# Power on GpSimd for the memory norms, an earlier order of the token norms, and memory attention by token halves, in a hybrid decoder layer

## The chip, the core and the metric

One core of one Trainium2 chip runs the whole layer in one launch. The time is that of the device in microseconds, the median of repeated runs of the same program; the profile is one further execution, recorded by the hardware profiler. The engines are named as in the profile: PE (TensorE), DVE (VectorE), ACT (ScalarE), POOL (GpSimd), and SP, whose queue issues the transfers here.

## The reference

One decoder layer on x of 1024 tokens by 1024 channels and a memory of 256 tokens, all float32:

```python
h = rmsnorm(x, norm_g)
pool_v, pool_gate, sb_q, sb_k, sb_v, sb_gate, mem_q, mem_gate = split(h @ w_in)
y_pool = pool_mixer(pool_v) * silu(pool_gate)
y_sb = stick_breaking_attention(sb_q, sb_k, sb_v) * silu(sb_gate)   # 8 heads of 64
mem_k, mem_v = split(rmsnorm(mem, mem_norm_g) @ w_mem_kv)
s = rmsnorm(mem_q, per head) @ rmsnorm(mem_k, per head).T * 64**-0.5  # 4 heads
y_mem = softmax(s) @ mem_v * silu(mem_gate)
out = x + concat(y_pool, y_sb, y_mem) @ w_out
```

An rmsnorm multiplies by (mean of squares + 1e-6) to the power -1/2. The pooling divides sums over windows of 2 to 16 tokens by the number of tokens in the window.

## The kernel before

Every product is made in three matmuls: an operand is split into a high part that ACT rounds and a low part that DVE or POOL gets by subtraction, and high by high, high by low and low by high are summed in PSUM. A projection of 128 output channels is a "unit" (u_q0, u_k0, u_v0, u_g0 for the first of four pairs of stick-breaking heads, and so on). It has two halves of 512 tokens, each of eight steps, one for each 128 input channels; a step is three matmuls of 512 columns (L208, L211). A unit's weights come through one single buffer, wr: SP loads it, ACT makes the high part (wh, L150), POOL the low part in four pieces (wl, L154), and only then can the next unit's load begin.

The program goes in stages:

- Start. The memory (m) is transposed and multiplied by its key and value weights (kv_step). Each of the eight token tiles (x0 to x7, 128 tokens each) is normalised: ACT squares and sums, DVE makes mean plus epsilon (root, L124), POOL raises it to -1/2 (L125), DVE refines it by a Newton step (L129, L130) and scales the tile (L135), or POOL scales it for tiles 4 and 5. h_step transposes one block of 128 channels of four tiles on PE (tx, L381), and ACT and DVE split it into hh and hl. A half needs all four of its tiles before its first block is done.
- Memory queries. The units mq0 and mq1 make four heads' queries into G0 to G3; ACT squares them (sqq), PE sums the squares of each head by a product with a matrix of two columns (sp, L553), and rsqrt_cols turns the sums into factors (qsc). The memory keys get the same norm (kv_root, kv_newton) and are transposed (km_step: tk on PE, then four operations on ACT and four on DVE).
- Memory attention (mem_main). It has 16 items, one for each pair of heads, head and 256 tokens. An item makes scores (z_m, L576, a bank of the two named z), their negative maximum on DVE (L578) and its product with qsc (L583), two exponentials on ACT (L587), the division of one half on POOL and one on DVE (L598), four transpositions (ta_m, L495), the split (ah_m, al_m), and the product with the values (av). The second use of a z bank waits for the exponentials of the item before the last.
- Four stick-breaking pairs (sb_main), whose chain runs from z over a sigmoid on ACT, a scan on DVE (L651), transpositions and splits to av; and then the output product.

In both attentions PE would wait for that chain. So `weave` mixes the items' steps (main) with steps of later units (fill): it takes fill steps until the time that its own cost table gives for the next main step, and leaves the last `keep` fill steps for the end. How many fill steps a stage gets is set by `cut`, and what is left goes to the first stick-breaking pair. PE's order is the program's order everywhere. The order of ACT, DVE and POOL is the program's up to start.close(), and is made by the scheduler of the framework from there on. Each engine works through its own list in that order, and an instruction that waits holds up those behind it.

Of the kernel before, what the change touches and what calls it, by code (L numbers as in the profile page):

```python
# [8 lines left out]
F32 = mybir.dt.float32  # L9
F32R = mybir.dt.float32r  # L10
AF = mybir.ActivationFunctionType
# [14 lines left out]
def layer_kernel(  # L26
# [56 lines left out]
    mhalf = const.tile([P, 1], F32, name="mhalf")  # L83
# [6 lines left out]
    def rsqrt_cols(ss, n, inv, name):  # L90
# [4 lines left out]
        nc.scalar.activation(t[:, :n], v[:, :n], AF.Sqrt)  # L95
        nc.scalar.activation(spare[:, 0:1], t[:, 0:1], AF.Copy)
        nc.vector.reciprocal(r[:, :n], t[:, :n])
# [464 lines left out]
    def mem_main(mq, ys):  # L562
        items = [(pr, h, j) for pr in range(2) for h in range(2) for j in range(NT // 2)]
        box = {}

        def qk(it):
# [15 lines left out]
            for i in range(2):  # L582
                nc.vector.tensor_scalar_mul(nb[:, 2 + i : 3 + i], nb[:, i : i + 1], qsc[:, c0 + 2 * i : c0 + 2 * i + 1])  # L583
# [197 lines left out]
    nc.scalar.activation(spare[:, 0:1], mhalf[:, 0:1], AF.Square)  # L781
# [3 lines left out]
    )  # L785
    warm(tm[0], 10)
# [12 lines left out]
    for kk in range(1, 4):  # L799
        xn[kk - 1].square()  # L800
        xn[kk - 1].root()
        kv_split(kk)
        xn[kk - 1].newton()
        xn[kk - 1].scale(nc.vector)
        if kk < 3:
            m_evac(kk + 1)
        kv_step(kk)
# [3 lines left out]
    xn[3].square()  # L811
    xn[3].root()
    xn[3].newton()
    xn[3].scale(nc.vector, slice(0, 512))
    w_mq = [(slot("wh", f"wh_mq{pr}", dt=F32R), slot("wl", f"wl_mq{pr}", dt=F32R)) for pr in range(2)]
# [25 lines left out]
    xn[4].square()  # L841
    xn[4].root()
# [13 lines left out]
    for k in range(KD):  # L856
        half[0, 0][k][1]()
        half[1, 0][k][1]()
        if k + 3 < KD:
            h_step(0, k + 3)  # L860
        if k >= 5:
            h_step(1, k - 5)
        if k == 0:
            for i in range(2):
                mn[i].newton(col=rm[:, i : i + 1])
        if k <= 3:
            xn[4 + k].newton()
        if k < 3:
            xn[5 + k].square()
            xn[5 + k].root()  # L870
        if k <= 3:
            xn[4 + k].scale(nc.gpsimd if k < 2 else nc.vector)
        if k == 3:
            u_q[0].weights()
        if k == 4:
            kv_evac()
# [10 lines left out]
    cnt = const.tile([P, 32], F32, name="cnt")  # L887
    for r in range(2):
        nc.gpsimd.iota(
            cnt[:, r * 16 : r * 16 + 16],  # L890
            pattern=[[1, 16]],
            base=1,
            channel_multiplier=0,
            allow_small_or_imprecise_dtypes=True,
        )
        for h in range(2):
            w = 2 << (2 * r + h)
            rows = slice(h * HD, (h + 1) * HD)
            nc.vector.tensor_scalar_min(cnt[rows, r * 16 : r * 16 + 16], cnt[rows, r * 16 : r * 16 + 16], float(w))
    nc.vector.reciprocal(cnt[:], cnt[:])  # L900

    for k in range(KD):
        half[0, 1][k][1]()
        half[1, 1][k][1]()
        if k == 0:
            kv_root()
            kv_newton()
        if k in (4, 5):
            km_step(kmn, k - 4)
        if k in (6, 7):  # L910
            mem_ss(k - 6, 0)
    mem_scale(0)
    start.close()
    fill = u_q[0].steps[8:] + chain([u_k[0], u_v[0], u_g[0], u_q[1], u_k[1], u_v[1], u_g[1]], u_q[2])
    cut = 8 + 16 + 17 + 16 + 3
    fill, fill_0 = fill[:cut], fill[cut:]
    run(fill[:6])
    mem_ss(0, 1)
    mem_ss(1, 1)
    mem_scale(1)  # L920
    nc.scalar.activation(spare[:, 1:2], spare[:, 0:1], AF.Exp, scale=0.0)
    run(fill[6:9])
    y_mem = [slot(f"Y{pr}", f"y_mem{pr}") for pr in range(2)]
    weave(mem_main(mq, y_mem), fill[9:], 6, 1.0)
# [227 lines left out]
```

## Time and profile before

| | us |
|---|---|
| median of three runs | 530.4 (529.99 to 531.61) |
| the profiled execution, whole | 531.56 |
| its span, first to last instruction | 529.6 |
| PE busy in the span | 514.6 |
| DVE busy | 392.9 |
| ACT busy | 292.0 |
| POOL busy | 173.0 |

The profiled execution lies 1.2 us above the median of the runs, and 2.0 us of it lie outside the span. The PE column counts matmuls as busy from start to end, overlapping ones once. A PE that is busy all the time may still go at the lower of its two clocks, which the granted clock shows: 1.00 is 2.4 GHz and 0.50 is 1.2 GHz.

### The profile page before, as it was taken

The numbers are of one execution on the slowest core, as the hardware profiler recorded it, in microseconds if no ns is written. First come the engines' busy times: TensorE is split into PE (matmuls) and PEld (weight loads), VectorE is DVE, ScalarE is ACT, GpSimd is POOL, SyncE is SP. The second block draws the span as 40 slices with busy tenths as digits, with TensorE's granted clock in tenths as the row PEclk, the third lists the DMA queues.
The fourth block names the chain that finished last, engine by engine and source line by source line (L and its number), as shares of the span: only waits on it lengthen the run. The fifth ranks groups of instructions, "written<-read, shape, count | busy, mean of one in ns | idle before, by whom it ended". The sixth has DMA issues, their size and how long they took to land.

```text
span 529.6 us, 7486 instructions
## 1 busy us (share of the span) xinstructions
PE 514.6 (97%) x2716; PEld 431.3 (81%) x2716; DVE 392.9 (74%) x654; ACT 292.0 (55%) x558; POOL 173.0 (33%) x193
## 2 busy tenths in 40 slices
PE   7899999899999999999999999999999999999997
PEld 6677788787888888888888888888788888888886
DVE  3776768787587764876766777647988859999863
ACT  6777666787565554555545564535544539462400
POOL 4770133543220322022302220222345920035890
PEclk9999989999999999999999999999999999999999
DMA  8911021301111310123011113100110415414023
GB/s 304 332 45 40 2 80 40 81 1 41 41 35 46 79 41 0 41 62 94 6 40 41 41 40 80 40 27 16 40 41 0 159 48 192 158 41 153 5 112 127
DMA packets 37245, 37.25 MB, mean 70 GB/s; under 512 B 1991, under 2 KB 26841, under 8 KB 37209
## 3 DMA queue, kind: packets, MB, share of 16 engines
q1 hardware_dynamic: 37208, 36.78, 22.3%
q8 instruction: 21, 0.34, 0.3%
q14 instruction: 16, 0.12, 0.1%
HBM read 28.39 MB, written 4.19 MB: 62 GB/s over the span
## 4 chain that ended last, share of the span: by engine, by line
PE 81%; DVE 9%; ACT 3%; issue 3%; POOL 2%; DMA 2%; SPq 0%; POOLq 0%; ACTq 0%; DVEq 0%
PE av L514 8%; PE z L643 7%; PE ta L495 6%; PE u_g L211 5%; PE u_q L211 5%; PE u_k L211 5%; PE u_v L211 5%; PE u_mg L211 3%; PE oS L1034 3%; PE oS L1036 3%; PE u_pv L211 3%; PE oS L1035 3%; PE u_q L208 3%; PE u_g L208 3%; PE u_k L208 3%
## 5 line engine op out<-in xcount | busy, mean ns | idle before, releaser
L651 DVE TENSOR_TENSOR_SCAN be<-be,later 128x128 f32<-128x128 f32 (+3 forms) x64 | 91.4, 1441 | 18.7 <-ACT be L647 17.9
L500 ACT ACTIVATE ah<-ta,mone 128x512 fp32r<-128x512 f32 (+1 forms) x80 | 51.7, 646 | 56.5 <-PE ta L495 55.8
L501 DVE SCALAR_TENSOR_TENSOR al<-ta,ah 128x512 fp32r<-128x512 f32 (+1 forms) x80 | 50.7, 634 | 24.9 <-ACT ah L500 23.9
L647 ACT ACTIVATE be<-z 128x128 f32<-128x128 f32 (+3 forms) x96 | 45.8, 490 | 35.7 <-PE z L643 34.2
L495 PE MATMUL ta<-ident,be 128*128 128x128 f32 x288 | 44.8, 273 | 0.0
L495 PEld LDWEIGHTS ta<-ident,be 128*128 128x128 f32 x288 | 35.1, 140 | 7.8 <-DVE be L651 0.4
L514 PEld LDWEIGHTS av<-ah,V_v 128*128 128x128 f32 x160 | 30.0, 188 | 7.0
L514 PE MATMUL av<-al,V_v 128*128 128x256 f32 (+1 forms) x160 | 31.7, 280 | 1.1 <-DVE al L501 1.1
L514 PE MATMUL av<-ah,V_v 128*128 128x256 f32 (+1 forms) x160 | 30.0, 269 | 0.0
L208 PE MATMUL u_g<-hh,wh_g 128*128 128x512 f32 x64 | 28.0, 438 | 0.0
L208 PE MATMUL u_v<-hh,wh_v 128*128 128x512 f32 x64 | 27.4, 427 | 0.0
L154 POOL TENSOR_TENSOR wl_g<-wr_g,wh_g 128x256 fp32r<-128x256 f32 x16 | 11.9, 779 | 45.9 <-ACT wh_g L150 45.9
L154 POOL TENSOR_TENSOR wl_k<-wr_k,wh_k 128x256 fp32r<-128x256 f32 x16 | 11.5, 751 | 46.7 <-ACT wh_k L150 46.7
L208 PE MATMUL u_k<-hh,wh_k 128*128 128x512 f32 x64 | 26.7, 417 | 0.0
L154 POOL TENSOR_TENSOR wl_v<-wr_v,wh_v 128x256 fp32r<-128x256 f32 x16 | 11.3, 741 | 45.7 <-ACT wh_v L150 45.7
L1034 PE MATMUL oS<-bs,hh 128*128 128x512 f32 (+1 forms) x68 | 25.9, 381 | 0.0
L1036 PE MATMUL oS<-bs,hl 128*128 128x512 f32 (+1 forms) x68 | 25.8, 379 | 0.0
L1035 PE MATMUL oS<-bs,hh 128*128 128x512 f32 (+1 forms) x68 | 25.6, 376 | 0.0
L598 POOL TENSOR_SCALAR pe_m<-pe_m,nb_m 128x256 f32<-128x256 f32 x16 | 16.3, 1019 | 28.0 <-DVE nb_m L595 20.5
L211 PE MATMUL u_v<-hl,wh_v 128*128 128x512 f32 x64 | 25.3, 396 | 0.0
L211 PE MATMUL u_k<-hh,wl_k 128*128 128x512 f32 x64 | 25.3, 395 | 0.0
L211 PE MATMUL u_g<-hl,wh_g 128*128 128x512 f32 x64 | 25.3, 395 | 0.0
(317 smaller groups left out, 1502.1 us busy)
## 6 DMA issues: line engine op xcount, KB each, us to landing
x<-in_x_dram SPq DMA_DIRECT2D x8, 512.0 KB, 6.3
wr_q<-in_w_in_dram SPq DMA_DIRECT2D x4, 512.0 KB, 4.8
wr_k<-in_w_in_dram SPq DMA_DIRECT2D x4, 512.0 KB, 3.8
wr_v<-in_w_in_dram SPq DMA_DIRECT2D x4, 512.0 KB
wr_g<-in_w_in_dram SPq DMA_DIRECT2D x4, 512.0 KB
KA_k<-KA_k SPq DMA_DIRECT2D x8, 256.0 KB, 5.3
KB_k<-KB_k SPq DMA_DIRECT2D x8, 256.0 KB
xr<-in_x_dram SPq DMA_DIRECT2D x8, 256.0 KB, 4.0
```

The source lines that it names most:

```text
L208: nc.tensor.matmul(pt[:], wh[:, kc], hh[k][:, c], start=(k == 0), stop=False)
L211: nc.tensor.matmul(pt[:], w[:, kc], h[k][:, c], start=False, stop=(k == KD - 1 and n == 1))
L495: nc.tensor.transpose(tp[:, o : o + P], src, ident[:])
L500: nc.scalar.activation(ah[:, :w], tp[:, :w], AF.Identity, bias=mone[:, 0:1])
L501: nc.vector.scalar_tensor_tensor(al[:, :w], tp[:, :w], -1.0, f(ah[:, :w]), op0=ALU.add, op1=ALU.subtract)
L514: nc.tensor.matmul(av[:, 256 - bw : 256], vs[n], part[:, o : o + bw], start=(first and part is ah and n == 0), stop=(last and part is al a ...
L643: nc.tensor.matmul(zp[:, 0:w], q[h][:, tcol], k[h][:, n, s0 : s0 + w], start=(n == 0), stop=(n == 1))
L647: nc.scalar.activation(be[:, s0 : s0 + w], zp[:, 0:w], AF.Sigmoid, scale=-(HD**-0.5))
L651: nc.vector.tensor_tensor_scan(be[:, rev], be[:, rev], mask, 1.0, op0=ALU.mult, op1=ALU.max)
L1034: nc.tensor.matmul(bk[:, c], xh[:, tcol], wh[:, c], start=(n == 0), stop=False)
L1035: nc.tensor.matmul(bk[:, c], xh[:, tcol], wl[:, c], start=False, stop=False)
L1036: nc.tensor.matmul(bk[:, c], xl[:, tcol], wh[:, c], start=False, stop=(n == 3))
```

## The change

It has five parts. The numbers of lines in the changed kernel differ by a few from those before.

1. rsqrt_cols (8 columns for the memory keys, 16 for each half of the memory queries) takes its power -1/2 on POOL in one instruction, where ACT took a square root and DVE a reciprocal. The activation tables that ACT had to load for this go, and so does the load for the exponential ahead of the memory attention: the first activation of the program is now an exponential.
2. The norms of the token tiles are put in another order: the square and the power of tile 3 stand ahead of the scaling of tile 2, those of tile 5 directly behind those of tile 4, and those of 6 and 7 one turn earlier. Eight transpositions of the identity into an unused bank (warm) stand ahead of the first h_step.
3. The counts for the pooling windows are made at the very start, and the sums of squares of the first half's queries and their factors stand ahead of the transposition of the memory keys instead of behind it.
4. The memory attention takes all items of the first 512 tokens first. The sums of squares and the factors of the second half's queries are no longer ahead of it but inside it, as two fill steps. The two products with qsc are one instruction of two columns.
5. The memory attention gets 72 fill steps, with the values of the second pair (u_v1) directly behind those of the first, where it had 51. The first stick-breaking pair has 50 projection steps left, where it had 64.

```diff
+    cnt = const.tile([P, 32], F32, name="cnt")
+    for r in range(2):
+        nc.gpsimd.iota(
...
+            nc.vector.tensor_scalar_min(cnt[rows, r * 16 : r * 16 + 16], cnt[rows, r * 16 : r * 16 + 16], float(w))
+    nc.vector.reciprocal(cnt[:], cnt[:])
     warm(tm[0], 10)
...
-        nc.scalar.activation(t[:, :n], v[:, :n], AF.Sqrt)
-        nc.scalar.activation(spare[:, 0:1], t[:, 0:1], AF.Copy)
-        nc.vector.reciprocal(r[:, :n], t[:, :n])
+        nc.gpsimd.tensor_tensor(r[:, :n], v[:, :n], mhalf[:, :n], op=ALU.pow)
...
-        items = [(pr, h, j) for pr in range(2) for h in range(2) for j in range(NT // 2)]
+        items = [(pr, h, 2 * th + j) for th in range(2) for pr in range(2) for h in range(2) for j in range(2)]
...
-            for i in range(2):
-                nc.vector.tensor_scalar_mul(nb[:, 2 + i : 3 + i], nb[:, i : i + 1], qsc[:, c0 + 2 * i : c0 + 2 * i + 1])
+            nc.vector.tensor_tensor(nb[:, 2:4], nb[:, 0:2], qsc[:, c0 : c0 + 3 : 2], op=ALU.mult)
...
-    nc.scalar.activation(spare[:, 0:1], mhalf[:, 0:1], AF.Square)
+    nc.scalar.activation(spare[:, 0:1], mhalf[:, 0:1], AF.Exp)
...
+    xn[2].square()
+    xn[2].root()
+    m_evac(3)
+    kv_step(2)
+    kv_split(3)
+    xn[2].newton()
+    xn[3].square()
+    xn[3].root()
+    xn[2].scale(nc.vector)
+    kv_step(3)
...
-    xn[3].square()
-    xn[3].root()
     xn[3].newton()
     xn[3].scale(nc.vector, slice(0, 512))
+    warm(ps("tr", "warm"), 8)
...
-    xn[4].square()
-    xn[4].root()
+    for i in (4, 5):
+        xn[i].square()
+        xn[i].root()
...
-        if k < 3:
-            xn[5 + k].square()
-            xn[5 + k].root()
+        if k < 2:
+            xn[6 + k].square()
+            xn[6 + k].root()
...
-        if k in (4, 5):
-            km_step(kmn, k - 4)
-        if k in (6, 7):
-            mem_ss(k - 6, 0)
-    mem_scale(0)
+        if k in (2, 3):
+            mem_ss(k - 2, 0)
+        if k == 4:
+            mem_scale(0)
+        if k in (5, 6):
+            km_step(kmn, k - 5)
     start.close()
-    fill = u_q[0].steps[8:] + chain([u_k[0], u_v[0], u_g[0], u_q[1], u_k[1], u_v[1], u_g[1]], u_q[2])
-    cut = 8 + 16 + 17 + 16 + 3
+    fill = u_q[0].steps[8:] + chain([u_k[0], u_v[0], u_v[1], u_g[0], u_q[1], u_k[1], u_g[1]], u_q[2])
+    cut = 8 + 16 + 17 + 17 + 16
     fill, fill_0 = fill[:cut], fill[cut:]
-    run(fill[:6])
-    mem_ss(0, 1)
-    mem_ss(1, 1)
-    mem_scale(1)
-    nc.scalar.activation(spare[:, 1:2], spare[:, 0:1], AF.Exp, scale=0.0)
-    run(fill[6:9])
+    run(fill[:9])
...
-    weave(mem_main(mq, y_mem), fill[9:], 6, 1.0)
+    def mem_late(n):
+        mem_ss(n, 1)
+        if n == 1:
+            mem_scale(1)
+
+    fill[13:13] = [(0.45, lambda: mem_late(0))]
+    fill[16:16] = [(0.45, lambda: mem_late(1))]
+    weave(mem_main(mq, y_mem), fill[9:], 4, 1.0)
```

Three places show how the instructions stand. First DVE at the norms of tiles 2 and 3; ss_x2 and ss_x3 hold the sums, and x2_99 and x3_100 are the tiles. Before:

```order
L130 TENSOR_SCALAR ss_x2_116<-ss_x2_116 128x1
L135 TENSOR_SCALAR x2_99<-x2_99,ss_x2_116 128x1024
L124 TENSOR_SCALAR ss_x3_117<-ss_x3_117 128x1
L129 TENSOR_SCALAR ss_x3_117<-ss_x3_117 128x1
L130 TENSOR_SCALAR ss_x3_117<-ss_x3_117 128x1
L135 TENSOR_SCALAR x3_100<-x3_100,ss_x3_117 128x512
```

Changed:

```order
L128 TENSOR_SCALAR ss_x2_116<-ss_x2_116 128x1
L122 TENSOR_SCALAR ss_x3_117<-ss_x3_117 128x1
L133 TENSOR_SCALAR x2_99<-x2_99,ss_x2_116 128x1024
L127 TENSOR_SCALAR ss_x3_117<-ss_x3_117 128x1
L128 TENSOR_SCALAR ss_x3_117<-ss_x3_117 128x1
L133 TENSOR_SCALAR x3_100<-x3_100,ss_x3_117 128x512
```

The mean of tile 3, on which POOL's power waits, is made ahead of the scaling of tile 2 instead of behind it.

Then ACT between the memory keys and the first exponential; km1 is the second pair's keys, G0 to G3 the queries, sqq their squares, wh_k0 and wh_v0 the high parts of the weights of the units k0 and v0. Before (the first exponential follows six rows below the last shown, behind the table load and the evacuation of u_q0):

```order
L478 ACTIVATE km1_670<-tk1_671,gcol_122 64x256 x4
L150 ACTIVATE wh_k0_788<-wr_k0_786 128x1024
L258 ACTIVATE G0_mq0_497<-u_mq0_1_597 64x512
L259 ACTIVATE G1_mq0_498<-u_mq0_1_597 64x512
L545 ACTIVATE sqq0_1_699<-u_mq0_1_597 128x512
L258 ACTIVATE G2_mq1_502<-u_mq1_1_601 64x512
L259 ACTIVATE G3_mq1_503<-u_mq1_1_601 64x512
L545 ACTIVATE sqq1_1_708<-u_mq1_1_601 128x512
L150 ACTIVATE wh_v0_800<-wr_v0_798 128x1024
L95 ACTIVATE t_q0_720<-v_q0_719 128x16
L96 ACTIVATE spare_72<-t_q0_720 128x1
L95 ACTIVATE t_q1_764<-v_q1_763 128x16
```

Changed, down to the first exponential, pe_m0_0_0:

```order
L476 ACTIVATE km1_705<-tk1_706,gcol_122 64x256 x4
L256 ACTIVATE G0_mq0_514<-u_mq0_1_606 64x512
L257 ACTIVATE G1_mq0_515<-u_mq0_1_606 64x512
L543 ACTIVATE sqq0_1_722<-u_mq0_1_606 128x512
L256 ACTIVATE G2_mq1_519<-u_mq1_1_610 64x512
L257 ACTIVATE G3_mq1_520<-u_mq1_1_610 64x512
L543 ACTIVATE sqq1_1_731<-u_mq1_1_610 128x512
L148 ACTIVATE wh_k0_768<-wr_k0_766 128x1024
L256 ACTIVATE qa0_q0_600<-u_q0_1_736 64x512
L257 ACTIVATE qb0_q0_601<-u_q0_1_736 64x512
L148 ACTIVATE wh_v0_780<-wr_v0_778 128x1024
L584 ACTIVATE pe_m0_0_0_796,nb_m0_0_0_794<-z_m0_0_0_789,nb_m0_0_0_794,qsc_151 128x256 x2
```

wh_k0 moves behind the six evacuations of the queries, and wh_v0 now stands directly ahead of the first exponential.

Last PE in the first items of the memory attention; u_k0 is the fill, z_m0_0_1 and z_m0_0_2 the scores of the second and third items, sp0_1 the sum of squares of the second half. Before:

```order
L576 MATMUL z_m0_0_1_830<-km0_652,G0_mq0_497 128x256 x4
L208 MATMUL u_k0_0_785<-hh3_83,wh_k0_788 128x512
L211 MATMUL u_k0_0_785<-hl3_91,wh_k0_788 128x512
L211 MATMUL u_k0_0_785<-hh3_83,wl_k0_789 128x512
L208 MATMUL u_k0_0_785<-hh4_84,wh_k0_788 128x512
L211 MATMUL u_k0_0_785<-hl4_92,wh_k0_788 128x512
L211 MATMUL u_k0_0_785<-hh4_84,wl_k0_789 128x512
L576 MATMUL z_m0_0_2_851<-km0_652,G0_mq0_497 128x256 x4
```

Changed, where the third item is z_m0_1_0:

```order
L574 MATMUL z_m0_0_1_812<-km0_687,G0_mq0_514 128x256 x4
L206 MATMUL u_k0_0_765<-hh4_84,wh_k0_768 128x512
L209 MATMUL u_k0_0_765<-hl4_92,wh_k0_768 128x512
L209 MATMUL u_k0_0_765<-hh4_84,wl_k0_769 128x512
L551 MATMUL sp0_1_829<-bones_76,sqq0_1_722 128x2 x4
L574 MATMUL z_m0_1_0_835<-km0_687,G1_mq0_515 128x256 x4
```

The first sum of squares of the second half has come to stand directly ahead of the third item's scores.

## Rows read from the trace of the kernel before

**Rows 1.** The windows view of the whole program by stage. Columns: stretch, its length, then for each engine the busy time in it (and instructions), the granted TensorE clock (1.00 is full), the DMA share and GB/s. 0 to 76.4 is the start with all norms and the memory keys, 76.4 to 138 the memory attention, 138 to 218 the first stick-breaking pair, 218 to 300 the second, 300 to 400 the third and the beginning of the fourth.

```profile
0.00:76.40 76.40, 68.87 (x328) 54.84 (x329) 49.83 (x121) 53.90 (x101) 33.15 (x53) 0.96 0.39 132
76.40:138.00 61.60, 58.43 (x348) 49.87 (x347) 46.76 (x123) 44.16 (x110) 23.49 (x29) 1.00 0.16 43
138.00:218.00 80.00, 80.00 (x448) 68.26 (x447) 56.40 (x77) 43.74 (x81) 15.60 (x22) 1.00 0.17 47
218.00:300.00 82.00, 82.00 (x461) 70.02 (x460) 58.37 (x80) 45.65 (x82) 15.54 (x23) 1.00 0.15 39
300.00:400.00 100.00, 98.89 (x539) 83.60 (x539) 76.48 (x109) 50.27 (x91) 24.22 (x26) 1.00 0.16 43
```

**Rows 2.** The view of who waited for whom, PE alone, whole program: in total, times, longest.

```profile
PE tx L381 <- DVE x L135: 2.9, 2, 1.7
...
PE av L514 <- DVE al_m L506: 1.9, 2, 1.6
```

**Rows 3.** The windows view, PE alone: stretch, length, PE busy (matmuls), granted clock, DMA share, GB/s.

```profile
22.60:24.30 1.70, 0.01 (x1) 1.00 1.02 407
...
24.30:28.30 4.00, 4.00 (x15) 0.57 0.19 72
...
72.80:76.50 3.70, 3.70 (x12) 0.60 0.02 4
```

**Rows 4.** Three rows of PE's timeline that begin behind a wait (start us, length us, engine, line, operation, out<-in, count, and in brackets the idle time before it and what ended it).

```profile
24.29 1.98 PE L381 MATMUL tx<-ident,x 128*128 128x128 f32 x9 [1.70 <-DVE x L135]
...
39.17 0.33 PE L381 MATMUL tx<-ident,x 128*128 128x128 f32 x1 [1.18 <-DVE x L135]
...
99.53 0.51 PE L514 MATMUL av<-al_m,vm 128*128 128x256 f32 x2 [1.57 <-DVE al_m L506]
```

**Rows 5.** DVE's timeline at the scaling of token tiles 2 and 3 (20.75 to 24.24) and of tiles 6 and 7 (35.07 to 39.11); same columns.

```profile
20.75 1.29 DVE L135 TENSOR_SCALAR x<-x,ss_x 128x1024 f32<-128x1024 f32 x1
...
21.95 0.14 DVE L124 TENSOR_SCALAR ss_x<-ss_x 128x1 f32<-128x1 f32 x1
...
22.76 0.27 DVE L129 TENSOR_SCALAR ss_x<-ss_x 128x1 f32<-128x1 f32 x1 [0.66 <-POOL ss_x L125]
...
23.26 0.98 DVE L135 TENSOR_SCALAR x<-x,ss_x 128x512 f32<-128x512 f32 x1
...
35.07 0.27 DVE L129 TENSOR_SCALAR ss_x<-ss_x 128x1 f32<-128x1 f32 x1 [0.96 <-POOL ss_x L125]
...
37.84 1.27 DVE L135 TENSOR_SCALAR x<-x,ss_x 128x1024 f32<-128x1024 f32 x1
```

**Rows 6.** One square of a token tile on ACT; same columns.

```profile
29.55 1.05 ACT L117 ACTIVATE sq_x<-x 128x1024 f32<-128x1024 f32 x1
```

**Rows 7.** PE's timeline through the end of the memory queries: a transposition of the memory keys (tk), the sums of squares (sp), the first projection step behind them, and one projection step with the first transposition of the memory attention (ta_m) behind it; same columns.

```profile
58.99 0.57 PE L471 MATMUL tk<-ident,kmn 128*128 128x128 f32 x2 [0.31 <-DVE kmn L449]
...
64.70 0.95 PE L553 MATMUL sp<-bones,sqq 128*128 128x2 f32 x8
...
65.83 0.51 PE L208 MATMUL u_q<-hh,w_q 128*128 128x512 f32 x1 [0.18 <-DVE ssb L555]
...
70.32 1.02 PE L553 MATMUL sp<-bones,sqq 128*128 128x2 f32 x8
...
71.69 1.25 PE L553 MATMUL sp<-bones,sqq 128*128 128x2 f32 x8 [0.35 <-DVE ssb L555]
...
83.58 0.40 PE L208 MATMUL u_k<-hh,wh_k 128*128 128x512 f32 x1
...
84.29 0.60 PE L495 MATMUL ta_m<-ident,pe_m 128*128 128x128 f32 x4
```

**Rows 8.** ACT's timeline from the memory keys (km) to the first exponential of the memory attention (pe_m); same columns.

```profile
61.60 1.92 ACT L478 ACTIVATE km<-tk,gcol 64x256 fp32r<-64x256 f32 x4
...
63.97 1.06 ACT L150 ACTIVATE wh_k<-wr_k 128x1024 fp32r<-128x1024 f32 x1 [0.45 <-PE u_mq L211]
...
65.05 0.59 ACT L258 ACTIVATE G_mq<-u_mq 64x512 fp32r<-64x512 f32 x1
...
71.67 1.06 ACT L150 ACTIVATE wh_v<-wr_v 128x1024 fp32r<-128x1024 f32 x1 [3.12 <-DMA wr_v<-in_w_in_dram]
...
78.03 0.56 ACT L587 ACTIVATE pe_m<-z_m,nb_m,qsc 128x256 f32<-128x256 f32 x1 [1.08 <-DVE nb_m L583]
```

**Rows 9.** The same timeline of POOL and of SP's queue: the low half of the first key weights, and the issue of the transfer that reuses their buffer.

```profile
65.11 2.81 POOL L154 TENSOR_TENSOR wl_k<-wr_k,wh_k 128x256 fp32r<-128x256 f32 x4 [6.75 <-ACT wh_k L150]
...
67.94 0.37 SPq L139 DMA_DIRECT2D wr_v<-in_w_in_dram  x1
```

**Rows 10.** Groups of POOL's instructions by line in the first 70 us: out<-in, shapes, count | busy us, mean ns of one | idle before. The first is a power with one column.

```profile
L125 POOL TENSOR_TENSOR ss_m<-ss_m,mhalf 128x1 f32<-128x1 f32 x2 | 1.1, 565 | 0.2 <-DVE ss_m L124 0.2
...
L730 POOL TENSOR_TENSOR pwr<-pw,pwr 128x128 fp32r<-128x128 f32 x1 | 0.5, 471 | 0.0
...
L160 POOL TENSOR_TENSOR w_kv<-raw,w_kv 128x512 fp32r<-128x512 f32 x1 | 1.3, 1297 | 0.0
```

**Rows 11.** The two activation table loads ahead of the memory attention, from the groups of ACT's instructions.

```profile
L95 ACT ACT_TABLE_LOAD x1 | 1.3, 1283 | 0.0
...
L921 ACT ACT_TABLE_LOAD x1 | 1.3, 1283 | 0.0
```

More of the change, by code (lines that the diff above doesn't have):

```diff
@@ L82, in layer_kernel @@
     rm = const.tile([P, 2], F32, name="rm")
-    mhalf = const.tile([P, 1], F32, name="mhalf")
+    mhalf = const.tile([P, 16], F32, name="mhalf")
     nc.gpsimd.memset(mhalf[:], -0.5)
@@ L785, in layer_kernel @@
     )
+    cnt = const.tile([P, 32], F32, name="cnt")
+    for r in range(2):
+        nc.gpsimd.iota(
+            cnt[:, r * 16 : r * 16 + 16],
+            pattern=[[1, 16]],
+            base=1,
+            channel_multiplier=0,
+            allow_small_or_imprecise_dtypes=True,
+        )
+        for h in range(2):
+            w = 2 << (2 * r + h)
+            rows = slice(h * HD, (h + 1) * HD)
+            nc.vector.tensor_scalar_min(cnt[rows, r * 16 : r * 16 + 16], cnt[rows, r * 16 : r * 16 + 16], float(w))
+    nc.vector.reciprocal(cnt[:], cnt[:])
     warm(tm[0], 10)
@@ L798, in layer_kernel @@
     kv_step(0)
[L799 to L807, printed above, removed]
+    xn[0].square()
+    xn[0].root()
+    kv_split(1)
+    xn[0].newton()
+    xn[0].scale(nc.vector)
+    m_evac(2)
+    kv_step(1)
+    xn[1].square()
+    xn[1].root()
+    kv_split(2)
+    xn[1].newton()
+    xn[1].scale(nc.vector)
+    xn[2].square()
[8 more added lines that the diff above has]
+    kv_step(3)
     raw_mq = [load_raw(w_in_v[:, :, 2560 + pr * P : 2560 + (pr + 1) * P], f"mq{pr}", early_raw[4 + pr]) for pr in range(2)]
@@ L886, in layer_kernel @@
             mq_late[pr][n]()
[L887 to L900, printed above, removed]
     for k in range(KD):
```

## The prediction

> **What bounds the kernel now.** I read the windows view by stages first. PE is busy for 80.0 of 80.0 us in the first stick-breaking pair and for all of the second, at full clock, while DVE has work for 70 to 71% of them (56.40 of 80, 58.37 of 82) [rows 1]. So the late stages are bound by PE's own work, which the change leaves as it is but for eight short transpositions. There is something to gain only where PE waits or goes at its lower clock: 76.40 - 68.87 = 7.5 us of waiting in the start and 61.60 - 58.43 = 3.2 us in the memory attention [rows 1].
>
> The waits view names the two places that weigh most, the scaled token tiles (2.9 us in two waits) and the low halves in the memory attention (1.9 us in two) [rows 2]. Behind the first tile wait the windows show a granted clock of 0.57 for 4.0 us, and of 0.60 for 3.7 us behind the sums of squares at 70 to 72 [rows 3]. PE is busy throughout in both, so they cost 4.0 x 0.43 = 1.7 and 3.7 x 0.40 = 1.5 us. Last I read the timelines of DVE, ACT and POOL at these places [rows 5, 8, 9], since each engine works off its list in order and the change moves the lists.
>
> **The change part by part.** Times are those of the profiled execution before, 531.56 us, 1.2 above the median of the runs; I subtract the sum from the median.
>
> *Tiles 0 to 3.* Before, the mean of tile 3 is made at 21.95, behind the scaling of tile 2 (20.75, 1.29 us), so DVE then stands for 0.66 us until POOL's power is back and ends the first half of tile 3 at 23.26 + 0.98 = 24.24 [rows 5]; PE goes on at 24.29 after 1.70 us [rows 4]. In the new order the power runs beside the scaling of tile 2. The pause of 0.66 goes, and the scaling itself, which had waited its turn behind POOL's power of tile 2, moves up by some 0.4: tile 3 is there 1.1 us earlier. The eight transpositions (0.7 us at the rate of the nine in [rows 4] at full clock) lie in what is left of the wait, so they cost nothing; without that cover they would cost their 0.7. The remaining pause is about half a us, shorter than the 1.18 us at 39.17 after which the clock stayed up [rows 4], so I expect full clock here.
>
> *Tiles 4 to 7.* The faster PE meets a chain that it does not speed up. Between PE's restart at 24.29 and its next tile wait, which ends at 39.17, lie 14.9 us of DVE work in order [rows 4, 5]. The earlier powers take out DVE's pause of 0.96 us before tile 6 [rows 5]. In its place the mean of tile 5, now directly behind that of tile 4, waits for a second square on ACT, 1.05 us long [rows 6], of which I take half. So tile 7 is scaled 1.1 + 0.5 = 1.6 us earlier than before, and PE waits there for about 2 us instead of 1.18. The gain of this stage is 1.6 us, and the 1.7 us of lower clock do not come on top of it: they turn into waiting for tile 7.
>
> *Norm of the keys and of the first queries.* Two table loads of 1.28 us each go from ACT [rows 11]. The first ran beside waiting for DVE, the second ended 2.6 us before the first exponential; only what PE waited for counts: 0.31 us before the keys' transposition and 0.18 behind the sums [rows 7]. I take 0.5 us. The counts for the pooling move to the start, where DVE has nothing to do.
>
> The price of POOL's power with 8 or 16 columns does not stand in the trace. One column takes 0.57 us [rows 10], so 16 take at least 0.57 and at most 16 x 0.57 = 9 us; an ordinary two-input instruction on POOL goes from 0.47 at 128 columns to 1.30 at 512, 2.2 ns a column [rows 10], which would leave the power at 0.6. A power is not an ordinary operation, and the only row of it is that of one column; I take 2.5 us, near the middle of the ends by ratio. Up to about 4 us the first two powers are hidden: the newly placed sums leave DVE idle until the keys come from ACT. The third, inside the memory attention, stands on POOL between the divisions of the second and third items, and DVE waits for it with the fourth item's scores behind it; up to some 3 us lie beside PE's fill. Beyond that each us costs one.
>
> The Trainium skill, in "GPSIMD Engine Reference", section 3.1, puts a two-input instruction at about 2.6 cycles an element, and its section 4.1 would keep elementwise work off this engine. The rows above agree for a subtraction (2.2 ns a column). By it all 16 columns would take about 0.6 us as an estimate, and the sum would stay as it is, since 2.5 is hidden too.
>
> *The first items of the memory attention.* Here the order of ACT speaks against the change. Let E be the end of PE's memory-query steps (65.83 before [rows 7]). In the changed order the second keys' block ends on ACT at about E + 1.0: it is transposed two steps before E, and follows four operations of 1.92 us. Then come six evacuations of 0.59 (E + 4.5), wh_k0 with 1.06 (E + 5.6), POOL's low half with 2.81 (E + 8.4), and only then the transfer of the next weights into the same buffer, 71.67 - 67.94 = 3.7 us [rows 8, 9] (E + 12.1), wh_v0 with 1.06 and two exponentials of 0.56 (E + 14.3). Before, wh_k0 stood ahead of the evacuations, and the same wait for the transfer (3.12 us) lay 5 us ahead of the first exponential [rows 8]. PE gets to the third item's scores, which need the bank of the first, after 13 steps of 0.70 (84.29 - 83.58 = 0.71 [rows 7]), two items' scores of two thirds of a step and one sum of 0.95: E + 11.0. So it waits there for 3.3 us.
>
> From there to the first transposition are four steps, two scores and a sum, 4.7 us, or E + 19.0. A wait that long, longer than the 1.70 that brought the lower clock, will bring it again [rows 3, 4]: 1.5 us more, E + 20.5. Before, this place is at 84.29 = E + 18.5 [rows 7], slow sums and lower clock included. The stage loses 2.0 us, or 1.5 with the 0.5 that E gains; what stands below as "entry" is -1.5.
>
> *The rest of the memory attention.* With 72 fill steps for 51, less two sums and a step of rounding, the stage gets about 14 steps more, 9.8 us of PE work over the same 16 chains. DVE has 46.76 us in 61.6 before, 76%; some 48 in 71 is 68%, under the 71% at which the second pair shows no wait [rows 1]. Of the 2.9 us that are left of the 3.2 (1.57 of them at 99.53 [rows 4]) I expect 0.5. Gain 2.4. Bounds: 2.9, and 0 if the waits stay.
>
> *The first stick-breaking pair* loses 14 steps: 70 us of PE work, and DVE's 56.4 less 2 for the values that moved, 77%. At 76% the third stretch of pairs has 1.1 us of waiting in 100, the memory attention 3.2 in 62 [rows 1]; the first is the same kind of work, so 0.8 us of loss, with 0 and 3.6 as ends.
>
> Sum: 1.6 - 1.5 + 2.4 - 0.8 = 1.7; 530.4 - 1.7 = 528.7 us.
>
> **The rivals.** (a) *The clock falls behind the wait for tile 7.* The wait of 2 us is longer than the 1.70 that brought it and than the 1.57 that did not [rows 4]; the gain of the start then goes: 1.6 more, 530.3. Against it: my estimate of the wait is uncertain by half a us.
> (b) *The power is paid per column*, 0.37 and more each, 6 us for 16. For: the only row is of one column. Then DVE stands for 3 us longer than PE's fill covers: 531.7. Against: nothing in the row says that its 0.57 are per column.
> (c) *Slower: the first pair is short of fill.* The 9.8 us that leave it were the cover of its chain of sigmoid, scan, transposition and split. If half of it opens as waits on DVE's results, 4.9 instead of 0.8, the time is 532.8. It decides from 4.1 us of waits in this stage. For: 77% of DVE is the highest share of all pairs. Against: the third stretch has nearly the same with 1.1 us [rows 1].
> (d) *Better: the third item's wait leaves the clock up, or is shorter,* because the transfer lands in less than 3.7 us or PE gets there later. Then 1.5 to 3 us less: about 526.6.
>
> **How the numbers follow.** The forecast has a chance of 0.36, with its own range 527.5 to 529.8; (a) 0.20, (b) 0.11, (c) 0.11, (d) 0.22. About 0.3%, 1.6 us, can be told from no change here. Faster than 528.8: 0.22 of the forecast, all of (d) and 0.03 of (a), 0.47. Slower than 532.0: 0.08 of (c), 0.05 of (b), 0.03 of (a), 0.16. The rest, 0.37, is the same. The range 525.5 to 532.3 takes in (a), (b) and (d), and leaves out most of (c) and the far end of (b).
>
> **What would show it.** Right: PE goes on after tile 3 near 23.2 at full clock, and after tile 7 near 37.5; ACT waits for wr_v0 directly ahead of the first exponential, and PE over 2 us for the third item's bank; after it almost no wait in the memory attention, and under 1 us in the first pair. Wrong: a power of 16 columns of over 4 us; no wait at the third item; waits of several us in the first pair.

## The result and the profile after

The changed kernel takes 532.57 us against 530.85 us, both medians of 20 runs on one chip: a ratio of 1.0029 with a 95% interval of 1.0018 to 1.0039. It is slower by just under 0.3%, where 528.7 in a range of 525.5 to 532.3 was forecast. The profiled execution has a span of 531.3 us against 529.6.

The windows view by the same stages as [rows 1]: the start now ends at 69.8, the memory attention at 148.5.

```profile
0.00:69.80 69.80, 63.59 (x319) 50.19 (x320) 46.83 (x110) 48.93 (x91) 33.98 (x49) 1.00 0.39 137
69.80:148.50 78.70, 73.49 (x408) 63.00 (x407) 49.51 (x118) 46.02 (x114) 33.21 (x42) 0.93 0.17 48
148.50:218.00 69.50, 69.44 (x393) 59.07 (x392) 52.88 (x71) 39.91 (x76) 11.96 (x16) 1.00 0.17 46
218.00:300.00 82.00, 82.00 (x460) 69.97 (x459) 58.33 (x79) 45.96 (x84) 13.91 (x21) 1.00 0.15 39
```

The start runs at full clock now (1.00 for 0.96). The mean clock of 0.93 in the memory attention is new. The waits view of PE, whole program, against [rows 2]:

```profile
PE z_m L574 <- ACT pe_m L584: 3.3, 1, 3.3
...
PE tv_v L306 <- DVE vt_v L298: 1.5, 2, 1.1
PE kv L412 <- DVE w_kv L158: 1.3, 1, 1.3
```

Both waits for scaled tiles are gone, and one of 3.3 us has come. PE's timeline around it (start, length, engine, line, operation, and in brackets the idle time ahead):

```profile
62.94 0.40 PE L206 MATMUL u_q<-hh,w_q 128*128 128x512 f32 x1
...
72.41 0.64 PE L574 MATMUL z_m<-km,G_mq 128*128 128x256 f32 x4
73.58 0.95 PE L551 MATMUL sp<-bones,sqq 128*128 128x2 f32 x8
77.85 1.22 PE L574 MATMUL z_m<-km,G_mq 128*128 128x256 f32 x4 [3.32 <-ACT pe_m L584]
81.43 1.70 PE L551 MATMUL sp<-bones,sqq 128*128 128x2 f32 x8
83.00 1.20 PE L574 MATMUL z_m<-km,G_mq 128*128 128x256 f32 x4
86.55 0.83 PE L493 MATMUL ta_m<-ident,pe_m 128*128 128x128 f32 x4
```

The memory queries end at E = 62.94, 2.9 us earlier than before [rows 7]. The first transposition of the attention (ta_m) stands at 86.55, 2.3 us later than before [rows 7]. So 5.2 us go between these two rows. The windows of PE alone show where a part of it goes:

```profile
70.00:77.00 7.00, 4.53 (x29) 0.98 0.26 77
77.00:87.00 10.00, 9.15 (x31) 0.50 0.18 52
87.00:90.00 3.00, 3.00 (x17) 1.00 0.00 0
```

For 10 us, from the end of the wait on, the granted clock is 0.50, the lower of TensorE's two levels (1.2 and 2.4 GHz). Who held the third item shows on ACT, against [rows 8], and on POOL:

```profile
67.58 1.06 ACT L148 ACTIVATE wh_k<-wr_k 128x1024 fp32r<-128x1024 f32 x1
...
75.52 1.06 ACT L148 ACTIVATE wh_v<-wr_v 128x1024 fp32r<-128x1024 f32 x1 [5.58 <-DMA wr_v<-in_w_in_dram]
76.60 0.56 ACT L584 ACTIVATE pe_m<-z_m,nb_m,qsc 128x256 f32<-128x256 f32 x1
```

```profile
68.72 2.81 POOL L152 TENSOR_TENSOR wl_k<-wr_k,wh_k 128x256 fp32r<-128x256 f32 x4 [7.76 <-ACT wh_k L148]
76.65 2.84 POOL L152 TENSOR_TENSOR wl_v<-wr_v,wh_v 128x256 fp32r<-128x256 f32 x4 [5.12 <-ACT wh_v L148]
79.47 1.95 POOL L595 TENSOR_SCALAR pe_m<-pe_m,nb_m 128x256 f32<-128x256 f32 x2
83.63 2.93 POOL L95 TENSOR_TENSOR r_q<-v_q,mhalf 128x16 f32<-128x16 f32 x1 [2.21 <-DVE v_q L94]
```

wh_k0 ends at 68.6, POOL's low half frees the buffer at 71.5, the transfer of the next weights lands at 75.5, and ACT stands for 5.58 us with the first exponential queued behind. POOL does the same once more: wl_v0 stands ahead of the first items' divisions.

From the first transposition to the second stick-breaking pair the changed kernel needs 61.95 + 61.47 us (148.50 and 209.97 are the first scores of the first and second pair) against 53.82 + 70.08 before: 0.5 less. Behind that the two kernels run in parallel, 1.6 to 1.8 us apart.

### The profile page after: what moved, and what is told of

It is laid out like the page before. It is cut to its first block, busy times and chain, and to the rows that moved or that the text cites. A ratio compares the mean times of both kernels' runs of the same rounds, so it can differ in the third digit from the quotient of the medians.

```text
span 531.3 us, 7462 instructions
## 1 busy us (share of the span) xinstructions
PE 515.5 (97%) x2724; PEld 431.9 (81%) x2724; DVE 392.6 (74%) x635; ACT 286.7 (54%) x549; POOL 178.9 (34%) x196
## 4 chain that ended last, share of the span: by engine, by line
PE 83%; DVE 6%; ACT 5%; issue 2%; DMA 2%; POOL 1%; SPq 0%; DVEq 0%; ACTq 0%; POOLq 0%
PE av L512 7%; PE z L640 6%; PE ta L493 6%; PE u_g L209 5%; PE u_k L209 5%; PE u_v L209 5%; PE u_q L209 4%; PE u_mg L209 3%; PE oS L1047 3%; PE oS L1049 3%; PE u_g L206 3%; PE oS L1048 3%; PE u_pv L209 3%; PE u_k L206 3%; PE u_v L206 3%; PE u_mq L209 2%
## 5 line engine op out<-in xcount | busy, mean ns | idle before, releaser
L209 PE MATMUL u_k<-hl,wh_k 128*128 128x512 f32 x64 | 26.2, 409 | 0.0
```

Source lines behind the costliest of these rows:

```text
L209: nc.tensor.matmul(pt[:], w[:, kc], h[k][:, c], start=False, stop=(k == KD - 1 and n == 1))
```

## The experiments

Each ratio is to the kernel before, timed beside it in five rounds, with the 95% interval; spans and instants are those of one profiled execution. The theory I formed from the profile was that the loss is the entry of the attention (the wait on wh_v0 and the low clock behind it); the main rivals were that it sits in the longer fill or the first pair, or that other queues set the pace anyway.

**1. The key unit's weights early.** The weights of u_k0 go into V1, free at that time, instead of the ring, ahead of the queries' evacuation.

```diff
+        if k == 4:
+            u_k[0].weights()
...
+    sb[0][1][1].tags = ("V1",)
```

> The changed kernel with the first key unit's weights split into the buffer V1 (free until the second value unit) ahead of the memory keys' evacuation, and not into the ring after it, so that the value unit's weights can be loaded some 5 us earlier; nothing else moves. Theory (the loss sits at the entry of memory attention: the third item's 3.32 us wait on wh_v0 and the 10 us of half clock behind it): wait under 0.5 us, granted clock stays at 1.0 from 70 to 90 us, the first transposed item comes 5 us earlier, time 5 to 6 us below the changed kernel, ratio to before about 0.992 (526.5 us). Rival (the loss sits later, in the longer fill's waits and the first stick-breaking pair; the entry is only the stretch in which it becomes visible): the time gained at the entry is waited for again before 210 us, ratio 1.000 to 1.003.

Ratio 1.0008 (0.9992 to 1.0023). The number lies in the rival's range, but the run tests neither. wh_v0 did run at 67.66 without a wait, but the scheduler now set the weights of the *next* unit into the freed ring, in the same place:

```profile
67.66 1.06 ACT L148 ACTIVATE wh_v<-wr_v 128x1024 fp32r<-128x1024 f32 x1
...
75.49 1.06 ACT L148 ACTIVATE wh_v<-wr_v 128x1024 fp32r<-128x1024 f32 x1 [5.53 <-DMA wr_v<-in_w_in_dram]
76.57 0.56 ACT L584 ACTIVATE pe_m<-z_m,nb_m,qsc 128x256 f32<-128x256 f32 x1
```

The wait stayed (2.94 us at the third item, first transposition at 86.53). The edit did not remove what it was meant to remove, so it says nothing against the theory.

**2. The second half's sums ahead of the first item.**

```diff
-    run(fill[:9])
+    run(fill[:7])
+    mem_ss(0, 1)
+    run(fill[7:8])
+    mem_ss(1, 1)
+    run(fill[8:9])
...
+    fill[16:16] = [(0.0, lambda: mem_scale(1))]
```

> The changed kernel with the second half's two groups of two-column sums moved ahead of the first item (between the last steps of the query unit), their powers left where they are. The wait of the third item on wh_v0 stays. Theory (the two-column sums inside the stretch after the wait keep the clock low): the wait is 3 us as before (the sums take the place of steps that stood ahead of it), but the half clock lasts 4 to 6 us instead of 10, ratio to before about 0.998 (529.8 us). Rival (the length of the half clock is set by the wait alone): half clock 10 us again, ratio 1.003.

Ratio 0.9991 (0.9977 to 1.0004): faster than the changed kernel, as the theory said. The wait at the third item was 3.73 us, put down to DVE, which had waited for POOL's power; the low clock was much shorter:

```profile
70.00:79.40 9.40, 5.67 (x30) 1.00 0.20 58
79.40:82.90 3.50, 3.50 (x11) 0.51 0.50 150
82.90:90.00 7.10, 7.10 (x42) 1.00 0.29 74
```

So a wait of much the same length is followed by 3.5 us of low clock here and by 10 there, where a group of two-column sums stands in the stretch. But the run moves the power too, and each of the two lengths is that of one execution: the mean clock of the twelve executions of this run goes from 0.993 to 0.997, that of the changed kernel's twenty from 0.989 to 0.997. So it is not shown that the sums prolong it.

**3. The wait filled.** 26 transposes of the identity ahead of the third item's scores.

```diff
+            if it == items[2]:
+                warm(ps("tr", "warm2"), 26)
```

> The changed kernel with 26 transposes of the identity (some 2.8 us by 0.107 us each) ahead of the third item's scores, where TensorE waits 3.32 us. Theory (the wait itself costs 3.3 us at most, the clock behind it 4.5 to 5): the items come at the same moments up to the third, the wait shrinks to about 0.5 us, the granted clock stays at 1.0, time 4 to 5 us below the changed kernel, ratio to before about 0.994. Rival (the half clock is the price of the sums or of the exponentials' pace, not of the idle engine): half clock as before, ratio 1.003 or more.

Ratio 1.0017 (1.0003 to 1.0031), an interval that overlaps the changed kernel's. The clock was 1.00 from 70 to 90 and 0.999 or more as a mean of each of the eleven executions, so with work in the wait it does not fall; but the gain expected of that did not come.

```profile
78.97 0.74 PE L576 MATMUL z_m<-km,G_mq 128*128 128x256 f32 x4 [1.36 <-ACT pe_m L586]
83.72 0.60 PE L493 MATMUL ta_m<-ident,pe_m 128*128 128x128 f32 x4
```

From the third item's scores to the first transposition it took 83.72 - 78.97 = 4.75 us, against 86.55 - 77.85 = 8.70: the low clock costs 4.0 us there. At the end 1.5 us of span were left between these two executions (by the ratios 0.6, not clear of noise): behind it PE waited 1.5 us for low halves, where the changed kernel has 0.4. The transfer also landed 1.1 us later in this execution. My theory that the clock was the larger half of the loss fell here.

**4. The new start with the old attention**: items head by head, 51 fill steps in the old order, sums and power ahead of the first item.

```diff
-    fill[13:13] = [(0.45, lambda: mem_late(0))]
-    fill[16:16] = [(0.45, lambda: mem_late(1))]
+    run(fill[:6])
+    mem_ss(0, 1)
+    mem_ss(1, 1)
+    mem_scale(1)
+    run(fill[6:9])
```

> The changed kernel with memory attention as before: items head by head, 52 fill steps in the old order of units, the second half's sums and power ahead of the first item; the power on GpSimd, the order of the token norms and of the memory keys stay. Theory (start and end of the memory queries gain 2.9 us, and the entry's stall is smaller here, since two groups of sums and one more step stand ahead of the third item): wait of 1 to 2 us at the third item, clock low for at most 4 us, ratio to before about 0.997 (529 us). Rival (the stall on wh_v0 belongs to the earlier end of the memory queries, not to the new order of attention): wait of 3 us or more and half clock of 10 us here too, ratio 1.002.

Ratio 1.0029 (1.0012 to 1.0046): the rival's case. E is 62.47, the wait at the third item 3.7 us, the clock 0.50 for 6.8 us (78.6 to 85.4), the first transposition at 86.0. So a loss of this size comes without the new order of attention too, though not by wh_v0 alone: the power stands ahead of the first item here (run 8).

**5. wh_v0 behind the third item's exponentials.** ScalarE is held to the written order over the first items, and the call for the value unit's weights is written six steps on.

```diff
-                a[0] = (KC, lambda f0=a[0][1], nxt=nxt: (f0(), nxt.weights()))
+                i = 6 if u is u_k[0] else 0
+                a[i] = (KC, lambda f0=a[i][1], nxt=nxt: (f0(), nxt.weights()))
...
+    hold = ExitStack()
+    hold.enter_context(tc.manual_schedule(engines={mybir.EngineType.Activation}))
+    fill[24:24] = [(0.0, hold.close)]
```

> The changed kernel with ScalarE held to the written order over the first items, and the call for the first value unit's weights written five steps later: wh_v0, which waits for its transfer, now stands behind the third item's exponentials and not ahead of the first. Theory (the head of ScalarE's queue sets the entry): no wait of TensorE at the third item (below 0.5 us), clock 1.0, the first transposed item at 78.5 to 80 us and not at 86.55, nearly all of it kept to the end: span 524 to 526 us, ratio to before 0.989 to 0.993. Rival (DVE and POOL set the pace of the items anyway, as the full clock of the run with transposes gained 2.9 us at the first transposed item and kept 1.5 of them): of 7 us at most 2 are kept, ratio 0.998 to 1.001.

**6. Both**: the weights early as in 1, and ScalarE in written order until the first value unit has begun.

> As the run before it, and the key unit's weights split early into V1, so that wh_v0 has its data at 67.7 us and stands where it stood, ahead of the first exponentials, without a wait; wh_v1 is kept behind the items by the written order. Theory (it was the wait for the transfer, not the place of the copy, that cost): no wait at the third item, first transposed item at 78.5 to 80 us, ratio 0.989 to 0.993, equal to the run before within 0.002. Rival: as there, 0.998 to 1.001; and if the copy's place on POOL's queue mattered (wl_v0 ahead of the first items' scaling there), this run is 1 us slower than the other.

Ratios 0.9955 (0.9937 to 0.9973) and 0.9932 (0.9917 to 0.9948). The fifth lies between the two ranges, the sixth at the upper end of the theory's. The sixth beats the kernel before by 0.68% and the changed one by 0.97%, 5.1 us. Its ACT and its PE:

```profile
67.50 1.06 ACT L148 ACTIVATE wh_v<-wr_v 128x1024 fp32r<-128x1024 f32 x1
...
73.02 0.56 ACT L584 ACTIVATE pe_m<-z_m,nb_m,qsc 128x256 f32<-128x256 f32 x1 [3.17 <-DVE nb_m L580]
```

```profile
74.62 0.72 PE L574 MATMUL z_m<-km,G_mq 128*128 128x256 f32 x4
76.57 0.95 PE L551 MATMUL sp<-bones,sqq 128*128 128x2 f32 x8
77.38 0.72 PE L574 MATMUL z_m<-km,G_mq 128*128 128x256 f32 x4
79.34 0.60 PE L493 MATMUL ta_m<-ident,pe_m 128*128 128x128 f32 x4
```

No wait at the third item, full clock, and the first transposition at 79.34 and not at 86.55: 7.2 us, of which 5.7 are kept at the second pair (204.31 for 209.97) and 5.6 in the span (525.7). The rival, that at most 2 would be kept, falls. In the fifth PE waits 2.9 us for low halves, with wl_v0 on POOL among the first divisions, and 1.0 in the sixth; the two intervals touch, so no difference between them is claimed.

**7. The sixth with the sums and the power ahead of the first item** (the edit of 2).

> As the run before it, with the second half's sums and its power ahead of the first item. The power (2.9 us) stands on POOL behind wl_v0, and DVE waits for it ahead of the first item's maximum. Theory (every wait ahead of the first exponentials passes to TensorE at the third item): wait of 0.5 to 1.5 us there, first transposed item at 81 to 83 us, ratio 0.993 to 0.996. Rival (sums ahead of the items are better in any case, since they keep two-column matmuls out of the entry): no slower than the run before it.

Ratio 0.9972 (0.9961 to 0.9984): slower than the sixth, against the rival. Not as I had put it, though: the ratio is above the 0.996 of the theory, the wait was not at the third item but between the two sums (1.4 us), the clock was at 0.50 from 71 to 78, and the first transposition came at 84.41.

**8. The fourth with the cure.**

> The kernel with memory attention as before (items head by head, 52 fill steps) and the new start, here with the key unit's weights split early and ScalarE in written order over the first items. Theory (the new start's loss without the new attention, 0.29%, was the wait for wh_v0): wait at the third item below 1.5 us instead of 3.7, first transposed item at 82 to 83.5 us instead of 86.0, ratio 0.994 to 0.997. Rival (the earlier end of the memory queries is worth nothing because attention is bound by other queues): ratio above 0.999.

Ratio 1.0016 (1.0006 to 1.0027). Missed: curing wh_v0 does not save the new start with the old attention. What took its place is the power:

```profile
68.39 2.77 POOL L152 TENSOR_TENSOR wl_v<-wr_v,wh_v 128x256 fp32r<-128x256 f32 x4 [4.98 <-ACT wh_v L148]
72.19 2.90 POOL L95 TENSOR_TENSOR r_q<-v_q,mhalf 128x16 f32<-128x16 f32 x1 [1.03 <-DVE v_q L94]
```

DVE waits 3.02 us for it ahead of every first maximum; PE waits 2.91 us between the sums and 1.23 at the third item. So in the fourth the power had its share in the wait too (ACT's first exponential waited there for DVE, 2.30 us behind wh_v0). The sixth differs from this run by parts 4 and 5 of the change and, by a little, in how long ScalarE keeps the written order: 1.0016 against 0.9932. How much of that lies in the place of the second half's norms, the seventh shows, which has the new attention with the norms ahead of it: 0.9972.

**9. The sixth with the power behind the sixth item.** GpSimd, too, is held to the written order here, over the same stretch as ScalarE.

> The fastest kernel so far (the changed kernel, the key unit's weights early, ScalarE in written order) with the second half's power moved on POOL from behind the second item to behind the sixth. In the run before it DVE waited there from 78.0 to 80.9 us, the fourth item's exponentials came only at 81.55, and TensorE stood for 1.0 us at the attention's first product. Theory (every wait of DVE at the entry is late at TensorE): that wait goes, span 1 us shorter, ratio 0.991. Rival (the 2.9 us of the power are only moved, and cost the same behind the sixth item): ratio 0.993 again.

Ratio 1.0030 (1.0018 to 1.0042): outside both.

```profile
89.88 2.93 POOL L95 TENSOR_TENSOR r_q<-v_q,mhalf 128x16 f32<-128x16 f32 x1
92.78 2.76 POOL L152 TENSOR_TENSOR wl_v<-wr_v,wh_v 128x256 fp32r<-128x256 f32 x4
```

```profile
97.29 0.79 PE L512 MATMUL av<-al_m,vm 128*128 128x256 f32 x2 [5.15 <-DVE al_m L504]
```

DVE stood 3.64 us for the power, then worked beside wl_v1 on POOL, and the low halves came 5.15 us late at PE. Here the wait of DVE in mid-attention cost more than the one at the entry. GpSimd's order moved as well (wl_v1 now directly behind the power), so the run does not part the two.

**10. The sixth without the eight added transposes.**

> The same kernel without the eight added transposes in the wait for the fourth tile of tokens (all else as there). Theory of the prediction (they are what keeps the clock up behind that wait): a stretch of half clock of about 4 us from 24 us on as in the kernel before, the end of the memory queries 1 to 2 us later (64 to 65 us), ratio 0.995 to 0.997. Rival (the tiles' earlier scaling makes the wait harmless): clock 1.0, end of the memory queries at 62.5 to 63 us, ratio 0.993.

Ratio 0.9932 (0.9917 to 0.9947), the rival's case to the digit:

```profile
24.08 1.20 PE L379 MATMUL tx<-ident,x 128*128 128x128 f32 x9 [0.70 <-DVE x L133]
```

```profile
22.40:24.10 1.70, 0.99 (x7) 1.00 1.03 410
24.10:28.30 4.20, 3.91 (x22) 1.00 0.17 61
```

The wait of 1.70 us before [rows 4] is one of 0.70, and the clock stays up without help. The transposes are worth nothing here: the ratio is that of the sixth.

**11. The sixth with the token norms in the order before**, and without the transposes.

> The same kernel with the token norms in the order of the kernel before, and without the eight transposes; the power on GpSimd, memory attention by halves and the cured entry stay. Theory (the start is worth 2 us and they are kept once the entry has no wait): end of the memory queries at 65 us, the rest behind it unchanged (141.5 us to the second stick-breaking pair), ratio 0.997. Rival (an earlier end of the memory queries is taken back by the load of the units' weights): the second pair starts at 204.3 us as with the new order, ratio 0.993.

Ratio 0.9973 (0.9961 to 0.9985), as the theory said. E is 66.23 against 62.67 in the tenth; from E to the second pair it is 141.48 us against 141.46, so once the entry has no wait all of a gain in the start is kept. The 3.6 us between these two profiled executions are not what the order is worth: this one is the slowest of its twelve, with low clock in the start,

```profile
26.80:30.30 3.50, 3.43 (x10) 0.51 0.11 31
```

which eight of the twelve do not have (mean clock 0.999 or 1.00). Those eight have a median span of 527.3 us, the tenth 525.5. So the order of the norms is worth 1.8 us at full clock, and 2.2 by the ratios.

**12. The kernel before with the cure alone.**

> The kernel before the change with the cure alone: the first key unit's weights split early into V1, and ScalarE in written order over the first items. There ScalarE waited 3.12 us for wh_v0 at 71.67 us, ahead of the square roots of the second half. Theory (in the kernel before this wait had room: TensorE stood for less than 1 us between the end of the memory queries and the first transposed item, so it takes the change and the cure together): gain of at most 1 us, ratio 0.998 to 1.001. Rival (the cure is worth its 5 us by itself, and the change is worth nothing): ratio 0.990 to 0.994.

Ratio 1.0007 (0.9990 to 1.0024). No difference: before the change the same wait for the transfer had room. The gain of the sixth belongs to the change and the cure together. The run shows one thing more. PE waits for tile 3 as long as in the profile before, and the clock stays up:

```profile
24.04 1.20 PE L381 MATMUL tx<-ident,x 128*128 128x128 f32 x9 [1.70 <-DVE x L135]
```

```profile
24.05:28.00 3.95, 3.66 (x21) 1.00 0.20 75
```

Before, the clock behind this wait was 0.57 [rows 3]. Up to there the two kernels are the same, so the same wait is followed by the low clock in one execution and not in another, and the prediction's line between waits of 1.57 and of 1.70 us does not hold.

## Why the prediction was wrong

The terms, from the profiled executions (plus is a gain):

| term | forecast | measured |
|---|---|---|
| start to E: tiles 1.6, norms 0.5 | +2.1 | +2.9 |
| E to the first transposition | -2.0 | -5.2 |
| rest of the memory attention | +2.4 | +1.2 |
| first stick-breaking pair | -0.8 | -0.7 |
| sum | +1.7 | -1.8 |

**The mechanism at the entry was seen, its size was not.** The wait of PE at the third item was put at 3.3 us and measured 3.32, with wh_v0 and its transfer ahead of the first exponential as forecast. The first failed step is the sentence behind it: "1.5 us more" for the lower clock. That price came from a stretch of 3.7 us [rows 3]. Here the low clock lasted 10 us and cost 4.0 until the first transposition (8.70 against 4.75 us in run 3 and 4.72 in run 6). The remaining 0.6 us came before it: the scores of the third item stood at E + 14.9 and not at E + 14.3. What sets the length stays open: 10 us here and in run 1, 6.8 in run 4, 3.5 in run 2, behind waits of 2.9 to 3.7 us, and other lengths in other executions of the same kernels.

**The second failed step is "Of the 2.9 us that are left ... I expect 0.5. Gain 2.4."** Run 3 shows it. With the clock up its first transposition stood at E + 20.6 (83.72, with E at 63.12), nearly the E + 20.5 of the forecast, and still it gained nothing on the kernel before. From there to the first pair it took 63.26 us, where 53.82 before and 9.3 of added work make 63.1: a gain of -0.1 and not 2.4. PE waited 3.0 us in this stretch,

```profile
PE av L512 <- DVE al_m L504: 1.5, 2, 1.0
PE tv_v L306 <- DVE vt_v L298: 1.5, 2, 1.1
```

and 3.1 us in run 6 (63.50 us long). The changed kernel has 1.9 us of waits there, and the +1.2 of the table. So with the entry as forecast the sum would have been about zero.

**The price at the first transposition is not the price at the end.** In eleven of the changed kernel's twenty executions the mean clock is 0.989 or 0.990, as in the profiled one, in seven 0.996 or 0.997. By an estimate from these means and the span that is 10 to 12 us of half clock and 3 to 4. The median spans are 531.1 and 529.7: the longer stretch costs 1.4 us of the span. The kernel before, timed beside runs 1 to 4, takes 528.6 at 0.996 or 0.997, so the change loses with the short stretch too. With the wait gone, 5.6 us came back (run 6). That the low clock partly covers other waits, because PE comes later to chains that are late anyway, fits these numbers and the longer waits of runs 3 and 6, but no run tests it by itself. For the changed kernel the cause of the loss is shown: the entry, with the wait on wh_v0 (runs 6 and 12).

**The start.** The gain came out near the 1.6 us forecast (1.8 to 2.2 by runs 10 and 11; the 2.9 of the table holds the low clock of the profile before), but not by the path forecast, so that is in part luck. Tile 3 was not earlier: PE took it up at 24.08 in run 10, against 24.29 before [rows 4], 24.04 in run 12 with the old order, and a forecast of 23.2. The power of tile 3 did run beside the scaling of tile 2, but took 1.11 us there, where the same power had taken 0.55 before, and DVE still stood for 0.44 us:

```profile
21.67 1.11 POOL L123 TENSOR_TENSOR ss_x<-ss_x,mhalf 128x1 f32<-128x1 f32 x1 [1.06 <-DVE ss_x L122]
```

```profile
22.82 0.27 DVE L127 TENSOR_SCALAR ss_x<-ss_x 128x1 f32<-128x1 f32 x1 [0.44 <-POOL ss_x L123]
```

For tile 7 there was no wait at all, where 2 us were forecast. PE came later, as it had not left tile 3 earlier, and the tile was ready at 37.1: DVE's scaling of it took 0.98 us, not 1.27 [rows 5].

```profile
36.14 0.98 DVE L133 TENSOR_SCALAR x<-x,ss_x 128x1024 f32<-128x1024 f32 x1
```

Wrong, too, was that "the faster PE meets a chain that it does not speed up". In run 12, with the old order and full clock, DVE scales tile 7 at 36.73 and not at 37.84 [rows 5]: of the 14.9 us that the prediction took as DVE's work it idled for 3.7, for ACT's halves behind PE's transpositions among others. Rival (a) fell. The eight transposes cost nothing, as said, and do nothing (run 10). A wait that I had not counted came with the new order, 1.30 us in the memory keys.

**The power on POOL.** 1.66 us for 8 columns and 2.90 to 2.93 for 16, against the 2.5 taken. With the 0.57 for one column [rows 10] that is about 0.16 us for each column more, so rival (b) had the mechanism right at less than half its price.

```profile
53.20 1.66 POOL L95 TENSOR_TENSOR r_k<-v_k,mhalf 128x8 f32<-128x8 f32 x1 [13.15 <-DVE v_k L94]
```

In the changed kernel DVE waits 1.60 us for the third power, and PE has no wait behind it until 100.11 (0.41 us). Where it stands ahead of the first items or in mid-attention it is not hidden (runs 8 and 9).

**The rest.** The count was off: 12 steps and two groups of transpositions went over to the attention, not 14 steps. (The stage has 67 fill steps and not 72, 16 more than before, and two of these are the sums; 72 - 51 less three would be 18. The 64 of the first pair before were 62 projection steps and two groups.) At 0.70 us a step [rows 7] and some 0.45 a group that is 9.3 us; the attention grew by 8.1 and the first pair shrank by 8.6, hence the table's +1.2 and -0.7. PE's waits in the attention went from 2.9 to 1.9 us and not to 0.5: two value units in a row brought one of 1.08 us for vt_v. Rival (c) needed 4.1 us of waits in the first pair; PE idled there for 0.06 us.

## What to carry to other kernels

When a stage ends earlier, look at what the engine's list holds next for the following stage: a copy that waits for a transfer at the head of ScalarE's list held every exponential behind it, and freeing a buffer let the scheduler put the next such copy into the same place. Compare a transfer's landing with the first use *behind it in the list*, not with its own use. And judge a stretch of low clock by what is left at the end when it is taken away, since other chains may be late in any case.

## What was not expected of the hardware

The power with 16 columns takes 2.9 us on GpSimd, as long as the subtraction of 1,024 columns in four pieces (2.8).

Some of DVE's instructions take longer while POOL subtracts. A 128x16 product took 0.69 us in run 9 at 92.85, beside POOL's four pieces, and 0.18 in run 6; a 128x16 operation with one input tile (L100) took 0.66 in run 8 at 62.09 and 0.17 in the changed kernel; the split of a key block took 1.73 us in the changed kernel and 0.68 before:

```profile
19.43 1.73 DVE L158 TENSOR_TENSOR w_kv<-raw,w_kv 128x512 fp32r<-128x512 f32 x1
```

```profile
19.12 0.68 DVE L160 TENSOR_TENSOR w_kv<-raw,w_kv 128x512 fp32r<-128x512 f32 x1
```

The first row is from the changed kernel, the second from before. POOL beside the first:

```profile
19.33 1.28 POOL L158 TENSOR_TENSOR w_kv<-raw,w_kv 128x512 fp32r<-128x512 f32 x1
```

The Trainium skill, in "SBUF — State Buffer", section "SBUF: two separate sides", says that DVE with two inputs in SBUF and GpSimd share a port pair that one of them holds for a whole instruction. The rows of the key block agree within 0.13 us: 0.68 us from the end of POOL's piece at 20.61 gives 21.29, and DVE's ended at 21.16.
